# RWKV-7 pairs in a hybrid layer: gram results and chain outputs kept twice, block matrices of a pair in 64 columns, their products per head in quarters of TensorE's array

## Chip, cores, metric

One core of one Trainium2 chip. The metric is the device time of one execution in microseconds (us). Three executions of the kernel before took 2756.22, 2758.50 and 2762.81 us; the median, 2758.5 us, is the number to compare with.

## What is computed

One layer of a streaming encoder for two groups of frames: 528 prompt frames (16 learned ones and 512) and 64 sample frames. Cut to what matters here:

```
h    = rmsnorm(x);  proj = h @ w_in              # 2048 -> 5936 columns
ya   = rwkv7_mix(proj[:, :3360])                 # 16 heads of 64, this change
yb   = mamba2_mix(proj[:, 3360:])
x    = x + [ya, yb] @ w_out
x    = x + (silu(h2 @ w_gate) * (h2 @ w_up)) @ w_down     # h2 = rmsnorm(x)

def step(S, (r, w, k, v, kk, ka)):               # rwkv7, per head, S is 64 x 64
    sa = S @ kk
    S  = S * w - outer(sa, ka) + outer(v, k)
    return S, S @ r
y = group_norm(y) * lnx_w + lnx_b + (sum(r*k*r_k) * v);  ya = y * g
```

The kernel does the recurrence in 10 chunks of 64 frames. Inside a chunk the steps depend on each other through a unit lower triangular 64x64 matrix, which is inverted; between chunks only S is handed on.

## The kernel before, in words

Big products (projections, output, feed-forward) are split products in fp32r: each 128x128 weight block is multiplied three times (high by high, high by low, low by high). A projected tile of 128 columns is 96 matmuls of 296 columns (`in_tile`, line 367), called mk (k), mr (r), mv (v), mz, mB, mC, mx, then mwo for `w_out`. Two tiles at a time have a slot of two banks, so a tile can begin only when the tile two before it has been taken out of its banks. The small products of the recurrence share three spare banks (`get`, line 250), and the chain has one of its own.

Beside these tiles run the small f32 products of the recurrence, one *pair* of heads at a time, pairs 0 to 7. The steps of pair j:

- `pre_r` (line 789) makes the decayed factors `KB` and `ST`; then 20 gram products gr of 64x128 by 64x128 (10 chunks, 2 heads). `gram_out` (line 770) masks and copies each: into `ST`, into the block matrices `GB`, the diagonal 32x32 blocks into `NX`, the off-diagonal ones into `NS`.
- the inversion of the 32x32 blocks: VectorE transposes `NX` to `NN` (128x1024, line 830), GpSimd runs 62 TENSOR_TENSOR steps, VectorE transposes the result to `Zc` (128x352, line 883). `ZM` and `YB` lie in the memory of `NN`.
- `solved` (line 880): products pm of `NS` by `ZM` join the halves; copies build the block matrices `Zd` and `MB`.
- `applied` (line 918): products pb = `Zd` by `GB`, a copy, products px = `MB` by that; the result goes to `PT` for the chain. `steps` (line 855) transposes `KB` (tr) into `GB` and `yb`.
- `chain` (line 984): 10 chunks one after the other; in each a product pair p with `ST`, copies, a product pair p with `PT`, updates; the output goes to `Y`.
- `post` (line 1034): group norm of `Y`, transposes into `yb`, gate.

All block matrices are [128 partitions, 10 chunks, 128 columns] with the two heads on the diagonal and zeros beside it, so one 128x128 product does both heads.

The order of all instructions on each engine is made while the program is built: every step is a generator, `beat` (line 215) advances those whose inputs a clock of the planner (`tick`, line 136, with a cost per operation in `Timed`) holds ready, and marks such as ("px", j, g) hold a step back. The engines then run their queues strictly in that order. Where the planner's clock and the chip differ, an engine waits at the head of its queue.

Of the kernel before, what the change touches and what calls it, by code (L numbers as in the profile page):

```python
# [17 lines left out]
P = 128  # L18
# [68 lines left out]
def tile_hybrid(ctx, tc, xt, wq, wg, wd, lrw, cst, vec, s0w, s0m, y_out, sh_out, wkv_out, cv_out, sm_out):  # L87
# [61 lines left out]
    class Timed:  # L149
# [5 lines left out]
        def __getattr__(self, op):  # L155
            f, e = getattr(self.eng, op), self.e

            def call(out, *a, **k):
                r = f(out, *a, **k)  # L159
                part = 0.1 * (out.shape[0] <= 64)  # L160
                if e == "PE":
                    n = out.free_size()
                    tick(e, n / 2400 + 0.0133 if a[1].dtype == F32R else 0.175 if op == "transpose" else max(0.218, 0.15 + n / 1100))
                else:
# [506 lines left out]
    pos_zv = pos[0]  # L671
    R, ses, MVs, st_o = {}, [], [], []
    hrow = [slice(0, 64), slice(64, 128)]
    vrow = [slice(64, 128), slice(0, 64)]

    def A2():
# [4 lines left out]
        R["KB"] = al2(1280, NC, P)  # L681
        R["GB"] = al2(1280, NC, P)
        R["NS"] = al2(640, 5, P)
        R["NX"] = al2(1024, 32, 32)
# [7 lines left out]
        MVs.append(al2(2 * NC))  # L692
        R["Y"] = al2(TR)
        ses.extend(al2(64) for _ in range(2))
        R["zd"] = p2[0]
        R["Zd"], R["MB"] = al2(1280, NC, P), al2(1280, NC, P)
        R["XX"] = al2(388)
        st_o.extend(al2(64) for _ in range(2))
        G.memset(R["NX"], 0.0)
        G.memset(R["NS"], 0.0)  # L700
        G.memset(R["Zd"], 0.0)
        unit()
        G.tensor_scalar(R["MB"], cc("idn").unsqueeze(1).broadcast_to([P, NC, P]), 1.0, None, ALU.mult)
        for h in range(2):
# [65 lines left out]
    def gram_out(j, h, c0, n, b, pg):  # L770

        yield "VA"
        gb_, st, kx = R["GB"], R["ST"][j % 2][h], 64 * h
        q, m = vrow[h], cc("m3")[:, 64 - 64 * h:192 - 64 * h]
# [6 lines left out]
        A.copy(R["NX"][hi, c0:c0 + n, :], pg[hi, 0:n, hi])  # L781
        A.copy(R["NS"][lo, c0 // 2:(c0 + n) // 2, hi], pg[lo, 0:n:2, hi])
        A.copy(R["NS"][hi, c0 // 2:(c0 + n) // 2, lo], pg[lo, 1:n:2, hi])
        put(b)
# [4 lines left out]
    def pre_r(j):  # L789
# [65 lines left out]
    def steps(j):  # L855
# [4 lines left out]
        for c0, n in groups:  # L860
            b = yield from get()
            pg = bank(b, f"tr{j}{c0}").rearrange("p (c x) -> p c x", x=P)
            for c in range(c0, c0 + n):
                PE.transpose(pg[:, c - c0, :], R["KB"][:, c, :], cc("idn"))
            if c0 == 8:
                mark(("Tm", j))
            yield "A"
            for h in range(2):
                A.copy(R["GB"][hrow[h], c0:c0 + n, hrow[h]], pg[hrow[h], 0:n, hrow[h]])
# [10 lines left out]
    def solved(j):  # L880
# [16 lines left out]
        for c in range(5):  # L897
            PE.matmul(pm[:, c, :], R["NS"][:, c, :], R["ZM"][:, c], start=True, stop=True)
        aside()
        for q in range(4):  # L900
            d = slice(32 * q, 32 * q + 32)
            for e, i0, i1, g in ((V, 0, 10, 3), (V, 10, 11, 2)):
                e.tensor_copy(R["Zd"][d, :, 32 * q + 3 * i0:32 * q + 3 * i0 + g * (i1 - i0)].rearrange("p c (i g) -> p c i g", g=g),
                              Zc[d, i0:i1, 0:10 * g].rearrange("p i (g c) -> p c i g", g=g))
        cur[0].aside = False
        yield "A"
        for h in range(2):
            lo, hi = slice(64 * h, 64 * h + 32), slice(64 * h + 32, 64 * h + 64)
            for par, q in enumerate((hi, lo)):
                A.activation(R["MB"][hi, par::2, lo], pm[q, :, 0:32], AF.Copy, scale=-1.0)  # L910
        put(b)
# [6 lines left out]
    def applied(j, g, c0, n):  # L918
# [115 lines left out]
    def post(j):  # L1034

        Y, MV, bon = c3(R["Y"]), MVs[0], bons[j % 2]
        yield from until(("post", j - 1), then="V")
# [6 lines left out]
        yield "A"  # L1044
        A.activation(yb, R["Y"], AF.Square)
        yield "V"
# [1118 lines left out]
```

## Time and profile before

| what | us |
|---|---|
| median of 3 executions | 2758.5 |
| the profiled execution, its own time | 2759.7 |
| its span in the trace | 2757.6 |
| TensorE busy in the span | 2646.3 (96%) |
| VectorE busy | 2187.0 (79%) |
| ScalarE / GpSimd busy | 1405.1 / 385.9 |

How to read it: the recurrence runs beside the projection tiles from about 155 to 840 us. Behind it come the Mamba part, `w_out` (from 1009 us) and the feed-forward part, which the change does not touch. A busy share of the whole span says little of the stretch in which the pairs run, so that one is read by itself.

### The profile page before, as it was taken

To read this page: it belongs to the slowest core of one execution; us is meant where nothing else is said; L and a number is where in the kernel's file an instruction comes from. 1 tells how busy PE (TensorE), PEld (TensorE's weight loads), DVE (VectorE), ACT (ScalarE), POOL (GpSimd) and SP (SyncE) were. 2 spreads that over 40 slices of the span, in tenths; PEclk is the share of its full clock that TensorE was granted. 3 is DMA by queue.
4 is the path that set the end of the run, shared out by engine and by line. 5 is a ranking of instruction groups with operands and counts; after the bars stand their busy time and mean duration, and the time that the engine had idled before them with its cause. 6 is when DMAs were issued, how large, how long until landed. Compare 5 with 4: busy or idle time off the path is not lost.

```text
span 2757.6 us, 51938 instructions
## 1 busy us (share of the span) xinstructions
PE 2646.3 (96%) x19236; PEld 2580.2 (94%) x19236; DVE 2187.0 (79%) x4216; ACT 1405.1 (51%) x3013; POOL 385.9 (14%) x673
## 2 busy tenths in 40 slices
PE   8998899989999999999999999999999989999997
PEld 7888789988998989999999999999999989999997
DVE  7675787878878675568898888889888868888885
ACT  5645565656555453454454444545444434444544
POOL 3224334443401120120000000000000000000004
PEclk9999799999999999999999999999999999999999
DMA  5421121222222344343344444444344385654623
GB/s 182 171 71 54 52 71 58 67 62 74 61 88 86 92 145 132 114 146 122 124 159 132 151 133 142 144 146 145 131 152 130 123 275 194 218 186 156 203 71 108
DMA packets 196461, 349.57 MB, mean 127 GB/s; under 512 B 26096, under 2 KB 102000, under 8 KB 196080
## 3 DMA queue, kind: packets, MB, share of 16 engines
q1 hardware_dynamic: 196208, 346.26, 39.0%
q8 instruction: 151, 2.47, 0.4%
q14 instruction: 102, 0.84, 0.1%
HBM read 281.13 MB, written 65.06 MB: 126 GB/s over the span
## 4 chain that ended last, share of the span: by engine, by line
PE 79%; DVE 5%; ACT 5%; POOL 3%; issue 2%; DMA 2%; DVEq 0%; SPq 0%; ACTq 0%; POOLq 0%
PE y L159 15%; PE a L159 14%; PE r L159 14%; PE x L159 7%; PE mwo L159 7%; DVE mem L159 4%; POOL mem L159 3%; PE mx L159 3%; ACT mem L159 3%; PE mv L159 3%; PE mk L159 2%; PE mr L159 2%; PE mz L159 2%; PE p L159 2%; PE me L159 2%
## 5 line engine op out<-in xcount | busy, mean ns | idle before, releaser
L159 ACT CAST memr<-mem 128x512 fp32r<-128x512 f32 (+2 forms) x1230 | 714.1, 586 | 900.2 <-PE y L159 208.2
L159 DVE TENSOR_TENSOR memr<-mem,memr 128x512 fp32r<-128x512 f32 (+2 forms) x1076 | 691.8, 648 | 262.0 <-ACT memr L159 257.4
L159 DVE TENSOR_TENSOR mem<-mem 128x576 f32<-128x576 f32 (+9 forms) x1016 | 696.9, 702 | 21.7 <-DMA mem<-x1d 10.8
L159 POOL TENSOR_TENSOR mem<-mem 128x84 f32<-128x84 f32 (+28 forms) x583 | 337.0, 579 | 2218.8 <-ACT mem L159 1553.8
L159 ACT ACTIVATE mem<-mem 64x64 f32<-64x64 f32 (+12 forms) x413 | 217.1, 534 | 174.6 <-DVE mem L159 155.1
L159 PE MATMUL y<-memr 128*128 128x288 f32 x1352 | 206.6, 300 | 15.3 <-DVE mem L159 15.3
L159 PE MATMUL mwo<-memr 128*128 128x288 f32 x1536 | 210.4, 298 | 0.0
L159 PEld LDWEIGHTS mwo<-memr 128*128 128x128 f32 x1536 | 205.9, 189 | 3.0 <-issue 2.5
L159 PEld LDWEIGHTS y<-memr 128*128 128x128 f32 x1352 | 192.2, 192 | 15.9 <-issue 15.9
L159 PE MATMUL r<-ffm,memr 128*128 128x288 f32 x1348 | 202.7, 297 | 1.6 <-DMA ffm<-pd 1.1
L159 PE MATMUL x<-memr 128*128 128x288 f32 x1352 | 201.4, 295 | 0.0
L159 PE MATMUL y<-ffm,memr 128*128 128x288 f32 x1356 | 201.2, 295 | 0.2
L159 PE MATMUL a<-memr 128*128 128x288 f32 x1352 | 199.7, 294 | 1.2 <-DVE memr L159 1.2
L159 PE MATMUL r<-memr 128*128 128x288 f32 x1352 | 199.1, 294 | 0.0
L159 PE MATMUL a<-ffm,memr 128*128 128x288 f32 x1328 | 197.1, 295 | 0.0
L159 PEld LDWEIGHTS r<-ffm,memr 128*128 128x128 f32 x1348 | 188.3, 190 | 2.8 <-ACT ffm L159 1.3
L159 PEld LDWEIGHTS y<-ffm,memr 128*128 128x128 f32 x1356 | 187.7, 188 | 0.7 <-DMA ffm<-pd 0.4
L159 PEld LDWEIGHTS a<-memr 128*128 128x128 f32 x1352 | 186.9, 188 | 1.4 <-DVE memr L159 1.4
L159 PEld LDWEIGHTS x<-memr 128*128 128x128 f32 x1352 | 187.8, 188 | 0.0
L159 PEld LDWEIGHTS r<-memr 128*128 128x128 f32 x1352 | 186.2, 188 | 0.0
L159 PEld LDWEIGHTS a<-ffm,memr 128*128 128x128 f32 x1328 | 183.9, 188 | 0.0
L159 PE MATMUL mk<-memr 128*128 128x296 f32 x768 | 125.3, 313 | 4.6 <-DVE mem L159 4.6
(184 smaller groups left out, 4051.6 us busy)
## 6 DMA issues: line engine op xcount, KB each, us to landing
mem<-in_wg SPq DMA_DIRECT2D x176, 512.0 KB, 3.4
mem<-in_wq SPq DMA_DIRECT2D x268, 256.0 KB, 2.7
mem<-in_wd SPq DMA_DIRECT2D x128, 320.0 KB, 3.3
pd<-mem SPq DMA_DIRECT2D x280, 144.0 KB, 2.0
memr<-pd SPq DMA_DIRECT2D x80, 288.0 KB, 6.3
ffm<-pd SPq DMA_DIRECT2D x60, 288.0 KB, 6.6
mem<-lrd SPq DMA_DIRECT2D x16, 320.0 KB, 3.8
mem<-in_xt SPq DMA_DIRECT2D x16, 296.0 KB, 5.7
```

The costliest lines, as they stand in the source:

```text
L159: r = f(out, *a, **k)
```

## The change

- `GB` and `NS` exist twice, taken by j mod 2. `pre_r` starts the grams of pair j when the transpose of `NX` of pair j-1 is issued (a new mark, "nt") and the products pb of pair j-2 are done; before, it waited for the products px of pair j-1.
- `Y` exists twice (the second is the old buffer `rs`). `chain` j waits for `chain` j-2's normalised output and for the last chunk of chain j-1; before, for the normalised output of j-1. `post` loads its gate into `bon` behind the addition that reads `bon`; before, into `rs` ahead of it.
- `Zd`, `MB`, `NS` are packed into 64 columns, each head's block in its own 64 partitions. The products pm, pb and px are issued per head: 64 rows by 64 columns of the array, 20, 20+20... in place of 10, 10, 10 per pair (pm: 5 to 10, pb: 10 to 20, px: 10 to 20).
- The planner's price of an f32 product whose stationary operand has 64 partitions is multiplied by 0.6; that holds for gr too.

```diff
-                    tick(e, ... max(0.218, 0.15 + n / 1100))
+                    tick(e, ... max(0.218, 0.15 + n / 1100) * (0.6 if a[0].shape[0] == 64 else 1))
...
-        R["GB"] = al2(1280, NC, P)
-        R["NS"] = al2(640, 5, P)
+        R["GB"] = [al2(1280, NC, P)]
+        R["NS"] = [al2(320, 5, 64) for _ in range(2)]
...
-        R["Y"] = al2(TR)
+        Ys.extend((al2(TR), rs))
...
-        R["Zd"], R["MB"] = al2(1280, NC, P), al2(1280, NC, P)
+        R["GB"].append(al2(1280, NC, P))
+        R["Zd"], R["MB"] = al2(640, NC, 64), al2(640, NC, 64)
...
-        yield from until(*[("px", j - 1, g) for g in range(3)], then="P")
+        yield from until(("nt", j - 1), *[("py", j - 2, g) for g in range(3)], then="P")
         for h in range(2):
...
         yield from until(*[("px", j - 1, g) for g in range(3)], then="V")
         V.transpose(NN, NX.rearrange("p c t -> p t c"))
+        mark(("nt", j))
...
         for c in range(5):
-            PE.matmul(pm[:, c, :], R["NS"][:, c, :], R["ZM"][:, c], start=True, stop=True)
+            for q in hrow:
+                PE.matmul(pm[q, c, :], R["NS"][j % 2][q, c, :], R["ZM"][q, c], start=True, stop=True)
...
         for c in range(c0, c0 + n):
-            PE.matmul(pg[:, c - c0, :], R["Zd"][:, c, :], R["GB"][:, c, :], start=True, stop=True)
+            for q in hrow:
+                PE.matmul(pg[q, c - c0, :], R["Zd"][q, c, :], R["GB"][j % 2][q, c, :], start=True, stop=True)
         mark(("py", j, g))
...
         for c in range(c0, c0 + n):
-            PE.matmul(pg[:, c - c0, :], R["MB"][:, c, :], yb_[:, c - c0, :], start=True, stop=True)
+            for q in hrow:
+                PE.matmul(pg[q, c - c0, :], R["MB"][q, c, :], yb_[q, c - c0, :], start=True, stop=True)
...
-        yield from until(("chain", j - 1), ("pb", j), ("v", j), ("T", j))
-        EC, st, Y = ECs[j % 3], R["ST"][j % 2], c3(R["Y"])
+        yield from until(("chain", j - 2), ("cl", j - 1), ("pb", j), ("v", j), ("T", j))
+        EC, st, Y = ECs[j % 3], R["ST"][j % 2], c3(Ys[j % 2])
...
-        load(rs, LRD[j, 2][:, 0:TR])
         V.tensor_scalar(yb, yb, vv("lw", j), vv("lb", j), ALU.mult, ALU.add)
         yield "V"
         V.tensor_tensor(yb, yb, bon, ALU.add)
+        load(bon, LRD[j, 2][:, 0:TR])
         yield "V"
-        V.tensor_tensor(yb, yb, rs, ALU.mult)
+        V.tensor_tensor(yb, yb, bon, ALU.mult)
```

The rest of the diff is the same buffers under `j % 2` and marks for pairs -1 and -2.

**VectorE, around the end of pair 0's inversion.** In the kernel before (gr10.. are the gram results of pair 1, p10 the chain of pair 0, the 128x352 transpose makes `Zc` of pair 0):

```order
L159 STREAM_TRANSPOSE mem2_1443<-mem2_1443 128x352
L159 COPY mem2_1443<-mem2_1443 32x165 x2
L159 TENSOR_TENSOR memr_62<-mem_61,memr_62 128x512
...
L159 TENSOR_TENSOR mem2_1443<-gr100_2345,mem_61 64x512
L159 TENSOR_TENSOR mem2_1443<-gr100_2345,mem_61 64x4x64
L159 TENSOR_TENSOR mem2_1443<-gr104_2354,mem_61 64x512
L159 TENSOR_TENSOR mem2_1443<-gr104_2354,mem_61 64x4x64
L159 TENSOR_TENSOR mem_61<-mv10_2174,mem_61 128x64
```

and in the changed kernel:

```order
L159 TENSOR_TENSOR mem2_1443<-gr100_2059,mem_61 64x512
L159 TENSOR_TENSOR mem2_1443<-gr100_2059,mem_61 64x4x64
...
L159 TENSOR_TENSOR mem2_1443<-gr118_2202,mem_61 64x256
L159 TENSOR_TENSOR mem2_1443<-gr118_2202,mem_61 64x2x64
L159 TENSOR_TENSOR mem_61<-mz50_2034,mem_61 128x296
L159 TENSOR_TENSOR mem_61<-mz51_2035,mem_61 128x296
...
L159 STREAM_TRANSPOSE mem2_1443<-mem2_1443 128x352
```

All gram results of pair 1 now stand ahead of the `Zc` transpose of pair 0; before, all stood behind it.

**TensorE, between the tiles mz4 and mv5.** In the kernel before:

```order
L159 MATMUL mz41_5275<-memr_62 128x296
L159 MATMUL p14_5496<-mem_61,mem2_1443 128x64 x2
L159 MATMUL gr508_5506<-mem2_1443 128x128 x2
...
L159 MATMUL tr50_5577<-mem_61,mem2_1443 128x128 x4
L159 MATMUL mv50_5591<-memr_62 128x296
```

and in the changed kernel (the beginning and the end of that stretch):

```order
L159 MATMUL mz41_5314<-memr_62 128x296
L159 MATMUL pm4_5486<-mem2_1443 64x33 x10
L159 MATMUL pb40_5509<-mem2_1443 64x128 x8
L159 MATMUL pb44_5518<-mem2_1443 64x128 x8
L159 MATMUL px40_5532<-mem2_1443 64x128 x8
L159 MATMUL px44_5544<-mem2_1443 64x128 x8
L159 MATMUL pb48_5553<-mem2_1443 64x128 x4
L159 MATMUL px48_5571<-mem2_1443 64x128 x4
...
L159 MATMUL p14_5583<-mem_61,mem2_1443 128x64 x2
L159 MATMUL bs50_5828<-mem_61 128x320
L159 MATMUL mv50_5830<-memr_62 128x296
```

26 small products stood between the two tiles; now there are 103, with all of pm, pb and px of pair 4 and 22 products of its chain. At the stretch between mv2 and mk4 it is the other way round: 63 before, 22 now.

## Rows read from the trace of the kernel before

**Rows 1.** The page's busy times of TensorE and VectorE in the span, and TensorE's granted clock in 40 slices of 69 us (tenths).

```profile
PE 2646.3 (96%) x19236; PEld 2580.2 (94%) x19236; DVE 2187.0 (79%) x4216; ACT 1405.1 (51%) x3013; POOL 385.9 (14%) x673
...
PEclk9999799999999999999999999999999999999999
```

**Rows 2.** GpSimd in order of time: the 62 steps of the inversion, pair by pair (start, length, in brackets the idle time before).

```profile
194.10 37.05 POOL L159 TENSOR_TENSOR mem<-mem 128x31 f32<-128x31 f32 x62 [45.05 <-DVE mem L159]
267.82 31.15 POOL L159 TENSOR_TENSOR mem<-mem 128x31 f32<-128x31 f32 x62 [35.20 <-DVE mem L159]
732.11 32.26 POOL L159 TENSOR_TENSOR mem<-mem 128x31 f32<-128x31 f32 x62 [35.03 <-DVE mem L159]
```

**Rows 3.** Busy time of the engines in the eight stretches from the `NN` transpose to the `Zc` transpose of a pair (pairs 0, 1 and 4, and the sum of all eight; start, end, length, then TensorE, weight loads, VectorE, ScalarE, GpSimd, granted clock).

```profile
191.90:231.20 39.30, 33.06 (x233) 32.02 (x232) 25.80 (x38) 15.76 (x30) 32.27 (x62) 0.97 0.30 92
265.60:299.70 34.10, 33.37 (x246) 32.02 (x245) 24.68 (x58) 16.32 (x48) 26.36 (x62) 1.00 0.21 56
498.90:536.40 37.50, 37.34 (x280) 36.29 (x279) 30.48 (x71) 20.12 (x58) 30.62 (x62) 1.00 0.18 52
sum 294.20, PE 282.32 PEld 270.31 DVE 217.25 ACT 144.77 POOL 231.04; mean PE 35.29 PEld 33.79 DVE 27.16 ACT 18.10 POOL 28.88
```

**Rows 4.** The same for the seven stretches between them, from the `Zc` transpose of a pair to the `NN` transpose of the next (the first, the second, the fifth, and the sum of all seven).

```profile
231.20:265.60 34.40, 32.19 (x218) 30.25 (x218) 16.23 (x42) 19.62 (x61) 0.74 (x2) 0.88 0.12 33
299.70:337.50 37.80, 30.05 (x156) 25.59 (x155) 31.63 (x66) 26.57 (x69) 0.74 (x2) 0.69 0.16 51
536.40:583.00 46.60, 38.75 (x258) 35.19 (x256) 36.40 (x76) 31.61 (x82) 0.73 (x2) 0.85 0.23 70
sum 278.30, PE 250.33 PEld 228.47 DVE 222.19 ACT 192.95 POOL 5.81; mean PE 35.76 PEld 32.64 DVE 31.74 ACT 27.56 POOL 0.83
```

**Rows 5.** VectorE's costliest forms from 150 to 770 us (busy us, mean ns of one, idle time before).

```profile
L159 DVE TENSOR_TENSOR memr<-mem,memr 128x512 fp32r<-128x512 f32 x106 | 75.2, 712 | 29.5 <-ACT memr L159 28.6
L159 DVE STREAM_TRANSPOSE mem<-mem 32x320 f32<-32x320 f32 x104 | 51.9, 499 | 2.0
L159 DVE TENSOR_TENSOR mem<-mem 64x640 f32<-64x640 f32 x62 | 51.4, 835 | 0.9
L159 DVE TENSOR_TENSOR mem<-gr,mem 64x512 f32<-64x512 f32 x32 | 22.0, 688 | 14.3 <-PE gr L159 13.9
L159 DVE TENSOR_TENSOR mem<-gr,mem 64x256 f32<-64x256 f32 x48 | 20.3, 422 | 3.4 <-PE gr L159 2.7
```

**Rows 6.** TensorE in order of time, pair 0: the end of pb and px, and the first grams of pair 1.

```profile
232.83 2.31 PE L159 MATMUL pm<-mem 128*128 128x33 f32 x10 [7.88 <-ACT mem L159]
241.16 1.95 PE L159 MATMUL px<-mem 128*128 128x128 f32 x16
242.94 0.61 PE L159 MATMUL pb<-mem 128*128 128x128 f32 x4
243.30 1.06 PE L159 MATMUL mv<-memr 128*128 128x296 f32 x6
244.20 0.61 PE L159 MATMUL px<-mem 128*128 128x128 f32 x4
245.55 1.16 PE L159 MATMUL gr<-mem 64*128 64x128 f32 x8
246.63 0.53 PE L159 MATMUL mv<-memr 128*128 128x296 f32 x2
247.09 1.16 PE L159 MATMUL gr<-mem 64*128 64x128 f32 x8
```

**Rows 7.** TensorE: two groups of gram products that follow each other, the first on one half of the rows, the second on the other; and a form with 112 and with 80 stationary columns (840 to 1060 us, count, busy, mean).

```profile
561.89 1.17 PE L159 MATMUL gr<-mem 64*128 64x128 f32 x12
562.99 0.66 PE L159 MATMUL p<-mem 128*128 128x64 f32 x4
...
L159 PE MATMUL yd<-mem 112*112 112x64 f32 x128 | 15.9, 286 | 4.6 <-DVE mem L159 4.6
L159 PE MATMUL yd<-mem 80*80 80x64 f32 x64 | 5.3, 236 | 1.2 <-DVE mem L159 1.1
```

**Rows 8.** TensorE between the tiles mv2 and mk4, the last and the first matmuls around it, and the last group before mv5.

```profile
305.49 1.07 PE L159 MATMUL mv<-memr 128*128 128x296 f32 x6
310.12 0.61 PE L159 MATMUL pb<-mem 128*128 128x128 f32 x4
313.77 0.85 PE L159 MATMUL px<-mem 128*128 128x128 f32 x4 [3.04 <-ACT mem L159]
342.17 0.99 PE L159 MATMUL mk<-memr 128*128 128x296 f32 x2 [0.15 <-DVE mem L159]
576.79 0.98 PE L159 MATMUL mv<-memr 128*128 128x296 f32 x2 [0.88 <-DVE mem L159]
```

**Rows 9.** VectorE: the tile mz4 is taken out of its banks, and mr6, whose banks mv5 needs.

```profile
563.65 0.83 DVE L159 TENSOR_TENSOR mem<-mz,mem 128x296 f32<-128x296 f32 x2
576.21 0.90 DVE L159 TENSOR_TENSOR mem<-mr,mem 128x64 f32<-128x64 f32 x3
```

**Rows 10.** TensorE in the Mamba part, around the first yd products behind mC1.

```profile
856.13 2.51 PE L159 MATMUL yd<-mem 112*112 112x64 f32 x16 [1.65 <-DVE mem L159]
860.53 0.90 PE L159 MATMUL mx<-memr 128*128 128x296 f32 x2 [1.89 <-DVE mem L159]
```

More of the change, by code (lines that the diff above doesn't have):

```diff
@@ L162, in call @@
                     n = out.free_size()
-                    tick(e, n / 2400 + 0.0133 if a[1].dtype == F32R else 0.175 if op == "transpose" else max(0.218, 0.15 + n / 1100))
+                    tick(e, n / 2400 + 0.0133 if a[1].dtype == F32R else 0.175 if op == "transpose" else max(0.218, 0.15 + n / 1100) * (0.6 if a[0].shape[0] == 64 else 1))
                 else:
@@ L671, in tile_hybrid @@
     pos_zv = pos[0]
-    R, ses, MVs, st_o = {}, [], [], []
+    R, ses, MVs, st_o, Ys = {}, [], [], [], []
     hrow = [slice(0, 64), slice(64, 128)]
@@ L699, in A2 @@
         G.memset(R["NX"], 0.0)
-        G.memset(R["NS"], 0.0)
+        for q in R["NS"]:
+            G.memset(q, 0.0)
         G.memset(R["Zd"], 0.0)
         unit()
-        G.tensor_scalar(R["MB"], cc("idn").unsqueeze(1).broadcast_to([P, NC, P]), 1.0, None, ALU.mult)
+        for q in hrow:
+            G.tensor_scalar(R["MB"][q], cc("idn")[q, q].unsqueeze(1).broadcast_to([64, NC, 64]), 1.0, None, ALU.mult)
         for h in range(2):
@@ L772, in gram_out @@
         yield "VA"
-        gb_, st, kx = R["GB"], R["ST"][j % 2][h], 64 * h
+        gb_, ns_, st, kx = R["GB"][j % 2], R["NS"][j % 2], R["ST"][j % 2][h], 64 * h
         q, m = vrow[h], cc("m3")[:, 64 - 64 * h:192 - 64 * h]
@@ L781, in gram_out @@
         A.copy(R["NX"][hi, c0:c0 + n, :], pg[hi, 0:n, hi])
-        A.copy(R["NS"][lo, c0 // 2:(c0 + n) // 2, hi], pg[lo, 0:n:2, hi])
-        A.copy(R["NS"][hi, c0 // 2:(c0 + n) // 2, lo], pg[lo, 1:n:2, hi])
+        A.copy(ns_[lo, c0 // 2:(c0 + n) // 2, 32:64], pg[lo, 0:n:2, hi])
+        A.copy(ns_[hi, c0 // 2:(c0 + n) // 2, 0:32], pg[lo, 1:n:2, hi])
         put(b)
@@ L868, in steps @@
             for h in range(2):
-                A.copy(R["GB"][hrow[h], c0:c0 + n, hrow[h]], pg[hrow[h], 0:n, hrow[h]])
+                A.copy(R["GB"][j % 2][hrow[h], c0:c0 + n, hrow[h]], pg[hrow[h], 0:n, hrow[h]])
             for h in range(2):
@@ L902, in solved @@
             for e, i0, i1, g in ((V, 0, 10, 3), (V, 10, 11, 2)):
-                e.tensor_copy(R["Zd"][d, :, 32 * q + 3 * i0:32 * q + 3 * i0 + g * (i1 - i0)].rearrange("p c (i g) -> p c i g", g=g),
+                e.tensor_copy(R["Zd"][d, :, 32 * (q % 2) + 3 * i0:32 * (q % 2) + 3 * i0 + g * (i1 - i0)].rearrange("p c (i g) -> p c i g", g=g),
                               Zc[d, i0:i1, 0:10 * g].rearrange("p i (g c) -> p c i g", g=g))
@@ L909, in solved @@
             for par, q in enumerate((hi, lo)):
-                A.activation(R["MB"][hi, par::2, lo], pm[q, :, 0:32], AF.Copy, scale=-1.0)
+                A.activation(R["MB"][hi, par::2, 0:32], pm[q, :, 0:32], AF.Copy, scale=-1.0)
         put(b)
@@ L933, in applied @@
         for c in range(c0, c0 + n):
-            PE.matmul(pg[:, c - c0, :], R["MB"][:, c, :], yb_[:, c - c0, :], start=True, stop=True)
+            for q in hrow:
+                PE.matmul(pg[q, c - c0, :], R["MB"][q, c, :], yb_[q, c - c0, :], start=True, stop=True)
         mark(("px", j, g))
@@ L1034, in post @@
     def post(j):
-        Y, MV, bon = c3(R["Y"]), MVs[0], bons[j % 2]
+        Y, MV, bon = c3(Ys[j % 2]), MVs[0], bons[j % 2]
         yield from until(("post", j - 1), then="V")
@@ L1044, in post @@
         yield "A"
-        A.activation(yb, R["Y"], AF.Square)
+        A.activation(yb, Ys[j % 2], AF.Square)
         yield "V"
@@ L1075, in tile_hybrid @@
         mark(("py", -1, g))
+        mark(("py", -2, g))
         mark(("px", -1, g))
-    for q in ("rk", "chain", "pb", "pre", "prek", "post", "kb", "T", "vd", "Tm", "cl"):
+    for q in ("rk", "chain", "pb", "pre", "prek", "post", "kb", "T", "vd", "Tm", "cl", "nt"):
         for i in (-1, -2):
```

## The prediction, made before the changed kernel ran

> **What bounds the kernel now.** I read the page first: TensorE is busy 96% of the span, VectorE 79%, and the granted clock is lowest in the slices from about 280 to 350 us [rows 1]. That is where the pairs run, so I then read GpSimd in order of time. It shows one inversion at a time, with a regular idle time of 35 to 45 us and always VectorE as the releaser [rows 2]. So the pairs follow each other in a fixed cycle, and I cut the stretch at two instructions of VectorE that each pair has once: the `NN` transpose, which starts the inversion, and the `Zc` transpose, which ends it. From the first `NN` (191.9 us) to the last `Zc` (764.4 us) that makes 572.5 us: 294.2 us in eight inversions [rows 3] and 278.3 us in the seven stretches between them [rows 4]. Two things are to be seen. In an inversion the time is GpSimd's (231.0 of 294.2 us busy; none is shorter than 34.1 us), while VectorE is busy for 217.3 us. Between them VectorE is the busiest beside TensorE: 222.2 of 278.3 us, and 36.4 of 46.6 us in the fifth. TensorE is busy 282.3 + 250.3 = 532.7 us of the 572.5, so it has 40 us left there. The cycle is therefore long because the inversion of pair j, then the copies, pm, pb, px and the grams of pair j+1 come one after the other: the first eight grams of pair 1 start at 245.55 us, 1.35 us behind the start of pair 0's last px group (244.20) [rows 6].
>
> **What the change could take away.** Grams of pair j+1 no longer wait for px of pair j. If their VectorE work moved into the inversion, the stretches between would shrink by what the grams cost VectorE. Whether it does is not a matter of the marks but of the order that the planner made, and there I counted, per stretch, VectorE's instructions with the mean duration of their form, of which the costliest stand in [rows 5]. In the order before, the counts of the eight inversions are 24.6, 24.0, 27.9, 27.4, 30.6, 28.1, 28.9, 24.0 (215.5 us) and of the seven stretches between 18.8, 34.3, 39.8, 40.3, 39.9, 38.2, 32.0 (243.3 us; more than the busy 222.2 since durations of neighbours overlap). In the changed order they are 29.6, 19.1, 25.0, 30.5, 21.5, 30.1, 26.9, 24.8 (207.5 us) and 11.7, 48.2, 43.1, 38.1, 39.1, 37.7, 35.2 (253.1 us). So only pair 1's grams move ahead of the `Zc` transpose of the pair before, as the first order rows show. For pairs 2 to 7 the grams' results still stand between `Zc` of pair j-1 and `NN` of pair j. They are held there by what was not doubled further: `ST` has two copies and waits for the chain of pair j-2, and the grams want the same three spare banks as pb and px.
>
> **The sum, by VectorE's cycle, against the profiled 2759.7 us.**
> - First stretch between: 34.4 us for a count of 18.8, so it waited [rows 4]. With a count of 11.7 it is bound by pm to px, which took from 232.83 to 244.81 us [rows 6]; with the 1.6 us from the `Zc` transpose (231.2) to pm, and some 0.9 us until the next `NN` transpose starts, that is 14.5 us. That is 19.9 us less.
> - The other six: 278.3 - 34.4 = 243.9 us for counts of 224.5, a factor of 1.086. New counts 241.4 by the same factor give 262.2 us: 18.3 us more.
> - The inversions: pair 1's was already at the 34.1 us floor. Pair 4's count falls from 30.6 to 21.5, so I let its 37.5 us fall to the floor: 3.4 us less. The others I leave.
> - Behind pm of pair 7: that product stands behind 3280 big matmuls before and behind 3272 now, so eight more are left, at 0.15 us each (mv x6 in 0.90 us) [rows 6]: 1.2 us more.
> - The first yd group of the Mamba part stood right behind mC1 and cost TensorE 1.65 + 1.89 us of waiting [rows 10]; it now stands 40 big matmuls later. I take half of that, 1.8 us less; below it could be nothing, above it the whole 3.5 us.
> - TensorE's own work. Quarters need the array in another tiling than the tiles around them. What such a visit costs the grams show: eight grams and two mv matmuls take 1.54 us (245.55 to 247.09), while at the prices around them (px x16 in 1.78 us, mv x6 in 0.90 us) they would take 0.89 + 0.30 = 1.19 us, so 0.35 us per visit [rows 6]. In the order the visits go from 45 to 75: 30 x 0.35 = 10.5 us. Against it pm gets cheaper. With 33 moving columns its price follows the stationary columns: yd takes 124 ns of busy time with 112 and 83 ns with 80 [rows 7], and the same slope gives about 62 ns at 64. Per pair ten records of 111 ns become ten of 62 ns in each head, side by side: 0.5 us less, 4 us in all. Net 6.5 us, in a stage in which TensorE has 40 of 572.5 us free. I charge half, 3.2 us; the ends are 0 and 6.5.
> - pb and px I cost at nothing more: two products on different rows of the array run side by side. In the group of 12 gram records that begins at 561.89 us the second head's start while the first's run, and all 12 leave in 1.10 us, with the change of tiling in it; one after the other at 111 ns they would need 1.33 us and the change on top [rows 7]. Quarters use different rows and different columns. If that cover is gone, it is the third rival.
> - The gate's load in `post` now follows the addition, so its landing is no longer hidden by two VectorE operations of some 0.8 us. Other steps' instructions stand between; the range takes 0 to 1.6 us per pair on VectorE, and I take 0, since `post` has no reader of that product in the cycle.
>
> Sum: -19.9 + 18.3 - 3.4 + 1.2 - 1.8 + 3.2 = -2.4 us, so 2757.3 us beside the profiled 2759.7. The profiled execution was 1.2 us above the median, so I predict **2756 us**. About 0.2% (5.5 us) is what a measurement of this kernel can tell from no change, so the forecast is no change.
>
> **Rivals.**
> 1. *The stretches between need less waiting, faster.* The grams made VectorE wait 13.9 + 2.7 us [rows 5], and the chains no longer wait for the group norm of the pair before. For it: those waits sit in the long stretches [rows 4]. Against: pairs 2 to 7 keep their place in the order, so the grams' waits stay likely. If the 16.6 us all go: 2756 - 17 = 2739 us.
> 2. *TensorE stalls between mz4 and mv5, slower.* mv5 needs the banks of mr6. Before, VectorE took mz4 out at 563.65 and mr6 at 576.21 us [rows 9], with a count of 9.5 us of work between them. Now the count is 35.2 us: the copies to `Zd`, the norm of pair 3, the decayed factors and the grams of pair 5 all stand ahead of mr6. At the same ratio (12.6 us for 9.5) that is 46 us without a big matmul, in which TensorE has 103 small products, some 16 us of work at 0.11 us a record: 30 us lost, where 15.5 - 5 = 10.5 us were lost. The stretch before mk4 gets better: 35.8 us (306.4 to 342.17) with 14 us of products in it [rows 8] becomes a count of 12.8 in place of 24.0 us, some 20 us with 4 us of products. Together that is 30 + 16 - 10.5 - 22 = 13.5 us more, and the 10.5 - 4 us of tiling are then not hidden: 2760 + 20 = 2780, less 1.2 us for the median, about 2779 us. It decides if TensorE, not VectorE's cycle, sets the pace: then what is lost there is not won back from the 40 free us. For it: TensorE is 93% busy in the stage. Against: VectorE would be working through that stall, so its cycle does not get longer by it.
> 3. *The quarters don't run side by side, slower.* Then 640 records of 111 ns stand where 320 stood: 35.5 us more of TensorE's work in pb and px. With half of it in TensorE's free time that is 18 us, else all: 2774 to 2792, say 2784 us. For it: the two grams that overlapped wrote two banks, and two quarters write the same bank, which no row shows. Against: they write different partitions of it. The Trainium skill, TensorEngine Tiling (Array Packing), section Gotcha 1: PSUM Pressure, says that different row tiles cannot access the same PSUM bank at once; by that rule the two heads' quarters take turns and this rival's time holds. The trace before neither confirms nor contradicts it.
>
> **How the numbers follow.** The forecast gets 0.50, with its own range 2748 to 2764 us; within it 0.17 falls below 2753, 0.26 between 2753 and 2764 and 0.07 above, as the sum lies on the faster side. Rival 1 gets 0.23, rival 2 0.16, rival 3 0.11. Faster: 0.17 + 0.23 = 0.40; the same: 0.26; slower: 0.07 + 0.16 + 0.11 = 0.34. The range 2733 to 2789 takes in the rivals' times with some 5 us beside them and leaves out a part of each end, less than 2 in 10.
>
> **What would show it.** Right: `NN` of pair 0 to `Zc` of pair 7 takes 560 to 580 us; the first stretch between is some 15 us, the second over 40; a stretch of over 35 us without a big matmul stands before mv5 and one of about 20 before mk4; a group pb x16 has become x32 in about the same 1.8 us. Wrong: pb x32 takes 3.5 us (rival 3); the seven stretches sum to under 265 us (rival 1); the 572.5 us grow by over 12 us with TensorE idle before mv5 (rival 2). If all stretches shrink together, the order was not what held the cycle, and the whole way of counting fails.

## The result: 1.0% slower, and the profile of the changed kernel

The changed kernel took 2786.7 us (median; 2784.5 to 2787.6), the kernel before 2760.7 us on the same chip. The medians give a ratio of 1.0094; the ratio on record, with its 95% interval, is 1.0101 [1.0088, 1.0115]. The forecast was no change, 2756 us. The profiled execution of the changed kernel took 2784.5 us, its span is 2782.7 us, 25.1 us more than before.

The page of the changed kernel, as in [rows 1]: busy times, and the granted clock in 40 slices.

```profile
PE 2665.5 (96%) x19636; PEld 2590.6 (93%) x19636; DVE 2186.3 (79%) x4216; ACT 1407.2 (51%) x3014; POOL 384.1 (14%) x675
...
PEclk9999889979999999999999999999999989999999
```

VectorE is as busy as before. TensorE is busy 19.2 us more and idle 5.9 us more. The granted clock is lower than before from 348 to 417 us and from 557 to 626 us, and a little higher from 278 to 348. The cut into stretches, as in [rows 3] (the inversions, pair 1 and the sum of eight) and then as in [rows 4] (the seven stretches between, each, and their sum):

```profile
240.40:275.90 35.50, 34.93 (x260) 33.71 (x260) 19.46 (x53) 17.70 (x51) 23.62 (x62) 1.00 0.20 54
...
sum 296.00, PE 285.79 PEld 273.99 DVE 210.91 ACT 159.03 POOL 231.79; mean PE 35.72 PEld 34.25 DVE 26.36 ACT 19.88 POOL 28.97
```

```profile
227.90:240.40 12.50, 12.01 (x140) 10.43 (x139) 9.39 (x19) 8.67 (x24) 0.79 (x2) 1.00 0.25 64
275.90:332.40 56.50, 48.39 (x350) 43.33 (x349) 44.27 (x101) 31.73 (x93) 0.73 (x2) 0.82 0.17 53
368.30:424.80 56.50, 49.73 (x325) 43.32 (x324) 40.04 (x87) 29.66 (x88) 0.73 (x2) 0.76 0.18 57
462.70:507.60 44.90, 42.43 (x337) 38.18 (x335) 34.74 (x67) 31.95 (x79) 0.87 (x2) 0.96 0.24 71
543.20:593.60 50.40, 35.05 (x221) 30.15 (x220) 36.58 (x81) 29.59 (x78) 1.06 (x2) 0.65 0.13 39
631.10:672.40 41.30, 39.05 (x326) 35.14 (x325) 34.74 (x75) 25.20 (x77) 0.72 (x2) 1.00 0.25 75
709.30:748.00 38.70, 37.73 (x323) 34.38 (x321) 32.54 (x72) 24.58 (x69) 0.73 (x2) 1.00 0.17 51
sum 300.80, PE 264.40 PEld 234.93 DVE 232.31 ACT 181.38 POOL 5.63; mean PE 37.77 PEld 33.56 DVE 33.19 ACT 25.91 POOL 0.81
```

From the first `NN` transpose (187.7 us) to the last `Zc` (784.5 us) it is 596.8 us, 24.3 more than the 572.5 before; what lies ahead of it got 4.2 us shorter and what lies behind 5.0 longer. So the loss lies in the cycle, in the stretches between: 300.8 against 278.3 us. The first fell to 12.5 us; two and three became the longest of all, 56.5 us each. VectorE is busy 10 us more there, and idle 68.5 in place of 56.1 us. What it waited for from the first `NN` to the last `Zc`, before and then changed (us in total, times, longest):

```profile
DVE mem L159 <- PE p L159: 36.8, 38, 2.5
DVE mem L159 <- ACT mem L159: 33.4, 31, 3.3
...
DVE mem L159 <- DMA mem<-lrd: 1.5, 3, 0.7
```

```profile
DVE mem L159 <- ACT mem L159: 52.8, 32, 5.3
DVE mem L159 <- PE p L159: 44.3, 36, 4.8
...
DVE mem L159 <- DMA mem<-lrd: 6.1, 4, 2.1
```

Two releasers grow, by 19.4 and 7.5 us. Most of both are round trips of the *chain*: a product p on TensorE, a hand-over by ScalarE, an update on VectorE, and back. The gate's load adds 4.6 us. So I read where each chain runs: its nine counted steps are the updates `mem<-p,mem,mem` 64x64. Before, the chains of pairs 1 and 2 ran from 336.5 to 371.5 and from 414.3 to 448.1 us, beside the inversions, with one step each ahead of the next `NN`: 35.0 and 33.8 us. In the changed kernel they begin at 305.2 and 393.8 us, 27 and 31 us ahead of the next `NN`, and take 50.0 and 52.0 us.

What such a step looks like, in the third stretch of the changed kernel, on VectorE (start, length, in brackets the idle time before):

```profile
401.67 0.60 DVE L159 SCALAR_TENSOR_TENSOR mem<-p,mem,mem 64x64 f32<-64x64 f32 x2 [1.52 <-PE p L159]
406.73 0.61 DVE L159 COPY mem<-p 64x128 f32<-64x128 f32 x2 [4.46 <-ACT mem L159]
407.37 1.12 DVE L159 TENSOR_TENSOR mem<-gr,mem 64x512 f32<-64x512 f32 x2
410.24 0.60 DVE L159 SCALAR_TENSOR_TENSOR mem<-p,mem,mem 64x64 f32<-64x64 f32 x2 [1.75 <-PE p L159]
```

and on TensorE and ScalarE meanwhile:

```profile
401.49 2.07 PE L159 MATMUL gr<-mem 64*128 64x128 f32 x8
403.50 1.43 PE L159 MATMUL bs<-mem 128*128 128x320 f32 x2
404.26 1.16 PE L159 MATMUL mv<-memr 128*128 128x296 f32 x2
405.22 0.95 PE L159 MATMUL p<-mem,mem 128*128 128x64 f32 x4
```

```profile
406.26 0.44 ACT L159 COPY mem<-p 64x64 f32<-64x64 f32 x2 [2.80 <-PE p L159]
```

VectorE's next instruction is the chain's copy, and behind it stand the grams that `NN` needs. The copy needs ScalarE, that needs the product p, and p stands behind grams, a bs group (other small products) and two mv on TensorE, at a granted clock of 0.50. So VectorE stands for 4.46 us. From 400 to 407 us it is busy 0.98 of 7.00 us.

### The profile page after: what moved, and what is told of

It is laid out like the page before. It is cut to its first block, busy times and chain, and to the rows that moved or that the text cites. A ratio compares the mean times of both kernels' runs of the same rounds, so it can differ in the third digit from the quotient of the medians.

```text
span 2782.7 us, 52739 instructions
## 1 busy us (share of the span) xinstructions
PE 2665.5 (96%) x19636; PEld 2590.6 (93%) x19636; DVE 2186.3 (79%) x4216; ACT 1407.2 (51%) x3014; POOL 384.1 (14%) x675
## 4 chain that ended last, share of the span: by engine, by line
PE 75%; DVE 8%; POOL 6%; ACT 4%; issue 3%; DMA 2%; SPq 0%; DVEq 0%; ACTq 0%; POOLq 0%
PE y L159 15%; PE a L159 14%; PE r L159 14%; PE x L159 7%; DVE mem L159 6%; PE mwo L159 6%; POOL mem L159 6%; PE mx L159 3%; ACT mem L159 2%; PE mv L159 2%; PE mk L159 2%; PE me L159 2%; PE mr L159 1%; PE p L159 1%; DVE memr L159 1%
## 5 line engine op out<-in xcount | busy, mean ns | idle before, releaser
L159 DVE TENSOR_TENSOR mem<-mem 128x1024 f32<-128x1024 f32 (+9 forms) x1008 | 690.8, 701 | 29.0 <-DMA mem<-x1d 10.7
L159 ACT ACTIVATE mem<-mem 64x64 f32<-64x64 f32 (+13 forms) x413 | 216.6, 533 | 201.4 <-DVE mem L159 179.3
L159 PEld LDWEIGHTS y<-ffm,memr 128*128 128x128 f32 x1356 | 187.7, 188 | 1.2 <-DMA ffm<-pd 0.7
L159 PE MATMUL mv<-memr 128*128 128x296 f32 x768 | 129.1, 318 | 3.4 <-DVE mem L159 3.4
## 6 DMA issues: line engine op xcount, KB each, us to landing
mem<-in_xt SPq DMA_DIRECT2D x16, 296.0 KB, 5.8
```

## The experiments

In all tables "chains 1, 2" are the lengths of the chains of pairs 1 and 2, "stretches" the sum of the seven from `Zc` to the next `NN`, and "last step" the last counted step of pair 7's chain, all from the profiled execution, in us. Before: 35.0, 33.8; 278.3; 839.6. Changed: 50.0, 52.0; 300.8; 857.8.

**First: which part.** The theories at the start were S (the stalls without big matmuls), Q (the products in quarters and their visits to the other tiling) and V (VectorE's cycle); from e5 on P (the place of the stall before mv5) and N (new work, wherever that stall stands: in e5 the quarters, from e6 on the second output's own edits).

e1, the planner's price for 64-row products as before; e3, grams wait for px of the pair before; e4, one chain output (the chain waits for the norm, the gate early in its own buffer). Lines are shortened to what differs:

```diff
e1 -max(0.218, 0.15 + n / 1100) * (0.6 if a[0].shape[0] == 64 else 1)
   +max(0.218, 0.15 + n / 1100)
e3 -until(("nt", j - 1), *[("py", j - 2, g) for g in range(3)], then="P")
   +until(*[("px", j - 1, g) for g in range(3)], then="P")
e4 -Ys.extend((al2(TR), rs))
   +Ys.extend([al2(TR)] * 2)
   -until(("chain", j - 2), ("cl", j - 1), ("pb", j), ("v", j), ("T", j))
   +until(("chain", j - 1), ("pb", j), ("v", j), ("T", j))
   -load(bon, LRD[j, 2][:, 0:TR])          # behind the addition
   +load(rs, LRD[j, 2][:, 0:TR])           # ahead of lw, lb
```

e2 is e1, e3 and e4 together: quarters and 64 columns alone. e5 is e1 and e4 together. e6 is the kernel before with e4's edit the other way round: the second output (with its late gate) alone.

> The changed kernel with the planner's old price (no factor 0.6), all else kept: two copies, 64 columns, quarters. Theory S (stall): what the change costs is TensorE's wait for the banks of the next tile, and it goes with the VectorE work that stands, in the order, between taking out the last tile and taking out the tile whose banks are needed next. Counted over the pairs' stage that is 52.7 us before, 71.7 us in the changed kernel, 32.5 us here. The change's 19 us of count cost 26 us, so 1.4 us per us: 20 us less than before gives about 28 us less, some 2733 us. Theory Q (tiling): the 30 more visits to another tiling cost the 26 us; here are 77 visits (75 in the changed kernel), so 2785 to 2790 us. Theory V (VectorE's cycle, as in the prediction): the counts give 569 us for the cycle, 3.6 us under the one before, about 2757 us.

> 64 columns and quarters alone: gram results, off-diagonal blocks and Y as in the kernel before (grams wait for px of the pair before, the chain for the norm before, second copies not needed), old price. 75 visits to another tiling, as in the changed kernel. Theory S: the count is 55.2 us against 52.7, so about 3 us more and 3 us for the tiling, some 2766 us. Theory Q: the whole 26 us, 2785 to 2790 us. Theory V: cycle 576 us, 2764 us.

> The changed kernel, but the grams of a pair wait for px of the pair before again (the second copies of the gram results are there and bring nothing). Theory S: the count is 58.6 us, 5.9 over before: about 8 us more, some 2768 to 2771 us. Theory Q: 73 visits, 2785 us. Theory V: cycle 582 us, 2770 us. If the early grams were what costs, this is the run that loses the 26 us; S says that it loses most of them, by its order alone.

> The changed kernel with one Y: the chain waits for the norm of the pair before, the gate is loaded into its own buffer early. Theory S: the count is 62.7 us, 10 over before: about 14 us more, some 2774 us. Theory Q: 74 visits, 2785 us. Theory V: cycle 571 us, 2759 us.

> The changed kernel with one Y and the planner's old price: of the change, quarters and two copies of the gram results are left. Theory P (place): the change's 26 us are one stall of TensorE's, in front of the tile mv5, which comes with the second Y; quarters and early grams by themselves cost under 5 us. Then this run stands with the one-Y run, 2750 to 2765 us. Theory N (new work): quarters cost some 20 us wherever they stand (as the run with quarters alone says, 2782), and early grams give back the 12 us that lie between the run whose grams wait (2798) and the changed kernel (2787): some 2770 us.

> The kernel before with the second Y alone (chain waits for the last chunk of the pair before and the norm of the one before that, the gate is loaded behind the addition). No quarters, no second gram results, old price. Theory P: the second Y costs by the stall that the order makes of it; here the order has 34 small products in front of mv5 (26 before, 103 in the changed kernel) and 57 in front of mk4 (63 before), so about the time before, 2755 to 2770 us. If the second Y costs by itself what lies between one Y and two in the changed kernel (30 us): 2790 us.

| run | us | ratio [95%] | chains 1, 2 | stretches | last step |
|---|---|---|---|---|---|
| e1 old price | 2768.7 | 1.0027 [1.0015, 1.0038] | 36.5, 38.2 | 295.6 | 838.4 |
| e2 quarters alone | 2782.2 | 1.0079 [1.0062, 1.0096] | 35.2, 44.9 | 309.0 | 853.9 |
| e3 grams wait | 2798.3 | 1.0134 [1.0119, 1.015] | 34.3, 34.3 | 330.8 | 875.7 |
| e4 one output | 2756.1 | 0.9978 [0.9968, 0.9988] | 33.7, 29.9 | 290.7 | 844.1 |
| e5 one output, old price | 2763.1 | 1.0009 [0.9998, 1.002] | 34.7, 35.8 | 294.6 | 841.8 |
| e6 second output alone | 2785.5 | 1.0103 [1.0082, 1.0123] | 33.3, 36.2 | 327.5 | 882.6 |

The part that costs is the second output: without it the change is 0.2% *faster* than before (e4), with nothing else it is 1.0% slower (e6; its profiled execution took 2793.1 us, so its stretches are read a little long). It does not cost alike in every order: with the old price and both outputs the loss is 0.27% (e1). The early grams do pay: 12 us (e3 against the change) and 19 us (e2 against e5). Q fell: e4 has 74 visits to the other tiling, the change 75, the kernel before 45. Yet quarters alone are 0.8% slower than before (e2), with the same visits, and why was not followed. No theory foresaw the times of e1 to e4: V came near in e4 alone (2759 us), Q in e2 alone (2785 to 2790), S in none. N's 2770 us for e5 was missed, where P's range held; in e6 it was N that came near.

**Is it the stall before mv5?** It came as rival 2 had it. Changed kernel: the last group of mz4, mv5's first (TensorE), mr6 taken out (VectorE), and that stretch:

```profile
541.91 5.70 PE L159 MATMUL mz<-memr 128*128 128x296 f32 x40
...
599.23 0.99 PE L159 MATMUL mv<-memr 128*128 128x296 f32 x2 [0.73 <-DVE mem L159]
```

```profile
598.66 0.89 DVE L159 TENSOR_TENSOR mem<-mr,mem 128x64 f32<-128x64 f32 x3
```

```profile
547.60:599.20 51.60, 34.20 (x199) 28.11 (x198) 36.62 (x80) 30.48 (x85) 2.86 (x9) 0.60 0.12 38
```

51.6 us without a big matmul against 15.5 before, at a granted clock of 0.60. e7 lets tile v5 take whichever of the two slots is free first; e8 is e4 with that rule for all tiles:

```diff
         s = mt[0] % nslots
         mt[0] += 1
+        if nslots == 2 and name == "v5":
+            stall(lambda: all(slots.get(q) == "busy" for q in (0, 1)), name)
+            s = min((q for q in (0, 1) if slots.get(q) != "busy"), key=lambda q: slots.get(q, 0.0))
         stall(lambda: slots.get(s) == "busy", name)
```

> The changed kernel, but the tile mv5 takes the slot that is free first (that of mz4) and not the one of mr6, which waits for VectorE. Up to the end of mz4 all orders are the same. Theory P: the stall of 51 us in front of mv5 falls to under 10 us; at the start of mk7 the kernel is 15 to 30 us ahead of the changed kernel (619.7 us). Behind it the order has another stretch of 66 small products, in front of mz7, that may take back half: 2765 to 2775 us. Theory N: the stall is only where new work shows, and the time stays within 5 us of 2787.

> The changed kernel with one Y, and every tile of the projections takes whichever slot is free first. In the order no stretch in front of a tile has over 24 small products but the chain's own. Theory P: no stall in front of a tile, so faster than before, 2735 to 2750 us. Theory N: 2756 (the one-Y run) or more.

e7: 2788.9 us, 1.0111 [1.0094, 1.0127]; mv5 begins at 551.0 us, 48 us sooner, and the time is that of the change. Chains 1 and 2 are unchanged, 50.0 and 52.0 us. The lead was given back at the tiles behind: mB begins 18 us ahead of the changed kernel (703.7 against 722.0 us), the first mx 2 us behind it. But e7 did not take such stretches away: two others came, of 27.8 us ahead of a mz and 14.4 ahead of a mC. Stretches of over 6 us without a big matmul, from 187 to 900 us, sum to 74.1 us in e7 and 83.5 in the changed kernel. What speaks against S and P is that this sum does not go with the time: it is 78.2 us in the kernel before and 29.4 us in e5, which takes as long. e8, made to have no long stretch ahead of a tile: 2785.3 us, 1.0104 [1.0083, 1.0125], 29 us slower than e4 and far from P's 2735 to 2750. So theories S and P fell; N is left, and what in it.

**Late gate, or early chain?** Two things come with the second output: the gate is loaded late (theory G), and the chain starts without the norm before it, ahead of the next `NN` (theory C). e9 is e4 and e10 the kernel before with the late load alone. e11 (the change) and e12 (e6) hold every chain behind the next `NN`:

```diff
e9, e10
+        load(bon, LRD[j, 2][:, 0:TR])      # behind the addition, in place of rs ahead of lw, lb
e11, e12
-        yield from until(("chain", j - 2), ("cl", j - 1), ("pb", j), ("v", j), ("T", j))
+        yield from until(("chain", j - 2), ("cl", j - 1), ("pb", j), ("v", j), ("T", j),
+                         *([("nt", j + 1)] if j + 1 < NPAIR else []))
```

> The kernel with one chain output (2756 us, the chain waits for the norm before it) with only the gate's load moved behind the bonus addition into the bonus's buffer, as the change has it. Theory G (the second output costs because it takes the gate's buffer: the gate then comes late, VectorE stands for its DMA at the end of every norm, 6.1 us in the changed kernel, and all that is queued behind stands with it): 2770 to 2788 us. Theory C (the second output costs because the chain, freed from the norm before it, starts ahead of the next pair's NN transpose, 17 of its 72 counted steps there against 8 before and 12 with one output, and each step is a round trip for which VectorE waits in order): 2756 to 2766 us, chain steps ahead of NN about 12.

> The kernel before with the late gate load alone (into the bonus's buffer, behind the addition); one output, chain waits for the norm. G: most of the +26 us that the second output with its late gate cost the kernel before, so 2774 to 2788 us. C: the waits on the DMA alone, 0 to 6 us more than before, 2759 to 2767 us.

> The changed kernel, two outputs and late gate kept, with one wait more: the chain of pair j also waits until the NN transpose of pair j+1 is issued. No chain step can then lie between Zc of a pair and the next NN. C: VectorE's stretches between fall from 300.8 us to 290 or less and the time to 2755 to 2768 us. G: the late gate stays, 2780 to 2792 us.

> The kernel before with the second output and the late gate (2785.5 us, 18 chain steps ahead of NN), and the same wait: the chain of pair j behind NN of pair j+1. C: stretches between from 327.5 us to under 300, 2755 to 2770 us. G: 2780 us or more.

| run | us | ratio [95%] | chains 1, 2 | stretches | last step |
|---|---|---|---|---|---|
| e9 one output, late gate | 2765.4 | 1.0009 [0.9997, 1.002] | 34.3, 29.2 | 282.1 | 844.9 |
| e10 before, late gate | 2782.5 | 1.0074 [1.0052, 1.0096] | 32.3, 39.7 | 315.4 | 867.1 |
| e11 change, chains held | 2757.5 | 0.9985 [0.9973, 0.9997] | 31.4, 30.7 | 285.1 | 839.2 |
| e12 e6, chains held | 2786.0 | 1.0085 [1.0065, 1.0106] | 30.1, 29.0 | 310.9 | 868.4 |

With the change, C is right: holding the chains takes the whole loss away, with both outputs and the late gate kept, and the late gate costs 9 us by itself (e9 against e4). With the grams, products and price of the kernel before, G's numbers came: the late gate alone costs 22 us, and holding wins nothing. G's mechanism is not shown by that. VectorE only waits 5 us more for the gate's DMA there; by count its queue holds 476 in place of 459 us of work from `NN` of pair 0 to `Zc` of pair 7, so the new order also moved other work into the cycle. What costs the rest stays open.

**Which chains.** e13 holds those of pairs 1 and 2, e14 of 4 to 6, e16 of 1, 2 and 4, e17 of 1 to 4. e15 is e4 with all held.

```diff
-        *([("nt", j + 1)] if j + 1 < NPAIR else []))
+        *([("nt", j + 1)] if j in (1, 2) else []))      # e14 (4, 5, 6); e16 (1, 2, 4); e17 (1, 2, 3, 4)
```

> The changed kernel with the chains of pairs 1 and 2 alone held behind the NN transpose of the next pair: the two that started 27 and 31 us ahead of it and took 50 and 52 us for their steps, against 29 to 41 us for the others. C (the early chains cost by their place): stretches two and three fall from 56.5 us each to 39 to 47, as with all chains held (45.1 and 39.5), and the time to 2758 to 2772 us. R (the run with all chains held was another order that happened to fall well, and no place is to blame): nothing says which half of it, the time anywhere from 2765 to 2795 us, and chains 1 and 2 not above 35 us long would go with no gain.

> The changed kernel with the chains of pairs 4, 5 and 6 alone held: they had 3, 2 and 2 steps ahead of NN and were 41.0, 40.7 and 38.8 us long. C: stretches two and three stay at 56.5, the gain is the smaller part, 0 to 10 us, so 2776 to 2787 us. R: anywhere from 2765 to 2795 us.

> The changed kernel with one output, the gate early in a buffer of its own and every chain held behind the next NN. If place of the chain and late gate add up: below both 2756 us (one output) and 2757.5 us (two outputs, held), 2742 to 2755 us. If holding and one output are two ways to the same thing (the chain does not start early): 2753 to 2762 us.

> The changed kernel with the chains of pairs 1, 2 and 4 held. With 1 and 2 alone held (2752.6 us) the chain of pair 4 had become the early one: 50.4 us long, four steps ahead of NN, stretch five at 56.0 us. C: that chain falls to under 35 us, stretch five below 52, and the time to 2742 to 2752 us. K (once the early chains are held, VectorE's count sets the stretches again: counts of the last six now 255.6 against 247.8, at the 1.106 that the last run had): 8.6 us more in the stretches, 2756 to 2768 us.

> The changed kernel with the chains of pairs 1 to 4 held. C: as with 1, 2 and 4 held, 2742 to 2752 us. K: counts of 247.0 in place of 247.8, so no change against 1 and 2 alone, 2749 to 2757 us.

| run | us | ratio [95%] | chains 1, 2 | stretches | last step |
|---|---|---|---|---|---|
| e13 held 1, 2 | 2752.6 | 0.9976 [0.9967, 0.9985] | 31.3, 30.9 | 286.6 | 832.8 |
| e14 held 4 to 6 | 2778.8 | 1.0080 [1.0060, 1.0099] | 49.8, 51.7 | 308.2 | 868.9 |
| e15 one output, all held | 2779.8 | 1.0079 [1.0064, 1.0094] | 29.7, 33.1 | 291.7 | 861.3 |
| e16 held 1, 2, 4 | 2751.6 | 0.9966 [0.9953, 0.9979] | 31.4, 30.7 | 292.3 | 836.2 |
| e17 held 1 to 4 | 2753.1 | 0.9973 [0.9962, 0.9984] | 31.4, 30.7 | 279.2 | 823.7 |

The two long chains are the cause in the changed kernel: holding them alone brings 34 us, more than C foresaw (2758 to 2772), and a kernel 0.24% faster than before; holding the later ones brings 8 at most. e13's stretches two and three:

```profile
276.40:321.40 45.00, 35.30 (x293) 31.37 (x291) 39.22 (x82) 28.88 (x72) 0.73 (x2) 0.88 0.21 64
356.50:396.20 39.70, 34.69 (x285) 30.33 (x284) 35.76 (x73) 23.73 (x66) 0.73 (x2) 0.91 0.21 61
```

84.7 us in place of 113.0: VectorE is busy 9.3 us less (the steps went beside the inversion, where GpSimd's time covers them) and idle 9.7 in place of 28.7 us. Of that idle time the chain's two releasers, p and ScalarE's mem, had 21.5 us in the changed kernel and 1.0 us in e13. Of the 32.5 us that the span got shorter, 17.4 lie in the cycle and 15.6 behind the last `Zc`. A chain step there on VectorE:

```profile
408.01 0.58 DVE L159 SCALAR_TENSOR_TENSOR mem<-p,mem,mem 64x64 f32<-64x64 f32 x2
408.51 0.60 DVE L159 TENSOR_TENSOR mem<-p,mem 64x128 f32<-64x128 f32 x2
409.04 1.66 DVE L159 SCALAR_TENSOR_TENSOR mem<-mem 128x640 f32<-128x640 f32 x2
411.40 0.60 DVE L159 SCALAR_TENSOR_TENSOR mem<-p,mem,mem 64x64 f32<-64x64 f32 x2 [0.69 <-PE p L159]
```

3.4 us from step to step, where the early chain took 8 to 9. Two things differ: the place and the clock. In e13 the granted clock is 1.00 from 408 us on, while those three early steps of the changed kernel (401.67 and 410.24 us are two of their ends) ran at 0.50 until 418 us. The early chain's fourth step, still ahead of `NN` and at full clock, took 3.5 us. But chain 4 of e13 has early steps of 8.4 and 6.4 us at full clock, with other work of VectorE between them. So a step can be long by its place alone, and no run says how much of the 8 to 9 us is the clock's.

Holding more chains wins nothing clear: in e16 K foresaw the stretches (last six 279.8 us for a count of 255.6) and missed the time (2751.6, C's range by its edge); in e17 K's range held. e15 missed both expectations: with one output and held chains, each chain waits for `NN` and for the norm before it, and pair 7's begins 55 us behind its `Zc` (41 us in e11). Of all kernels here, those up to 2769 us have their last chain step at 824 to 845 us, those from 2778 us on at 852 to 883.

**What stays open.** Early and long chains of pairs 1 and 2 are what the changed kernel pays for, but they are not the only way to lose such a time, and not every early chain is a loss. e2, e3, e6, e8, e10, e12 and e15 took 2780 to 2798 us with chains 1 and 2 of at most 45 us, in e8, e12 and e15 with no step ahead of `NN`. In e13 the chain of pair 4 is early and 50.4 us long, with four steps ahead of `NN`, and the kernel is faster than before; holding that chain too (e16) wins 1 us by the medians, 3 by the ratios. VectorE stood only 5.7 us for that chain's two releasers in the stretch, and TensorE kept its clock (0.95):

```profile
516.80:572.70 55.90, 52.22 (x406) 47.72 (x405) 44.01 (x94) 32.08 (x91) 0.73 (x2) 0.95 0.24 76
```

In stretches two and three of the changed kernel VectorE stood 21.5 us for them, and the clock was 0.82 and 0.76. The mean granted clock of the profiled executions parts the two groups as the last step does: 0.964 to 0.972 from 2778 us on, 0.973 to 0.977 up to 2769 us (before, changed, e13):

```profile
core 0: 2757.6 us, clock 0.974
core 0: 2782.7 us, clock 0.968
core 0: 2750.2 us, clock 0.977
```

With two levels, 0.50 and 1.00, that is some 143, 178 and 127 us at the lower one. Eight grams take 2.07 us there and 1.16 at full clock (below), so the 35 us more of the changed kernel are worth up to some 15 of its 25 us, an estimate from these rows. In the stretch read below TensorE waited before the clock fell, so the clock need not be a cause of its own; no run holds it fixed, and its share stays open.

## Why the prediction was wrong, point by point

The frame held: 24.3 of the 25.1 us lie between the first `NN` and the last `Zc`, and the first stretch fell by 21.9 us (19.9 forecast). The forecast had taken it from rows of which the first, up to 239 us, ran at a granted clock of 0.50 [rows 6]; in the changed kernel that stretch has 1.00.

**The step that failed is "the other six ... by the same factor give 262.2 us".** The order was counted rightly and the factor was wrong: 288.3 us for a count of 241.4 is 1.194, not 1.086. That is 26.1 us, nearly the whole miss of 27.5 us (2.4 us less forecast, 25.1 more measured). The factor is no constant of the engine; it holds waiting in it, and the place of a chain is one thing that decides how much. By stretch, for two and three: changed 56.5/48.2 = 1.17 and 56.5/43.1 = 1.31, together 13.8 of the 26.1 us; with the two chains held 45.0/42.4 = 1.06 and 39.7/38.0 = 1.04. Most of the rest is in stretch five, 50.4/39.1 = 1.29, with three steps of chain 4 ahead of `NN`, and in stretch four, 44.9/38.1 = 1.18, with none of chain 3, so that one the early chain does not explain. For the last six: 1.106 in e13, 1.102 in e11, 1.080 in e17. With the early chains held the factor of before is a fair one again in these three. The prediction had the order in which it could have been seen: it counted the work in a stretch, not the round trips in it.

- *Rival 1* took the opposite side of the same edit: "the chains no longer wait for the group norm". That wait was the thing that kept the chain behind the grams. VectorE did wait less for grams (7.5 in place of 12.2 us) and more for chains.
- *Rival 2*: its stall came (51.6 us; 46 forecast), and so did the shorter one before mk4 (17 us, some 20 forecast). That stall is not what is paid: in e7 it is gone and the time is the same. What it says of TensorE setting the pace is not refuted: of the 25.1 us, TensorE is busy for 19.2, with hardly more work and a lower clock.
- *Rival 3*: fell. pb and px of pair 0 in the changed kernel, as in [rows 6], and pm ahead of them:

```profile
230.28 0.74 PE L159 MATMUL pm<-mem 64*64 64x33 f32 x18 [0.20 <-DVE mem L159]
...
236.32 1.96 PE L159 MATMUL px<-mem 64*64 64x128 f32 x32
238.12 0.60 PE L159 MATMUL pb<-mem 64*64 64x128 f32 x8
```

  32 quarters px take 1.96 us where 16 full products took 1.95; pb x32 takes 2.37 us in pair 0 and 1.96 in pair 3, where 16 took 1.95 to 2.22. The Trainium skill, TensorEngine Tiling (Array Packing), section Gotcha 1: PSUM Pressure, says that different row tiles cannot access the same PSUM bank at once; the measurement decides, and here two quarters on different rows and columns wrote one bank at no loss in px.
- *The inversions*: 296.0 us, 5.2 over the forecast. Pair 4's fell to 35.6, not to the floor of 34.1.
- *Tiling visits*: 3.2 us charged. No run has the visits alone: e4 with 74 is faster than before, but with the early grams; e2 with 75 and without them is slower. So the term is neither borne out nor refuted.
- *pm*, forecast 0.5 us a pair cheaper: its 20 quarters take 1.20 or 1.21 us from first to last in five of the eight pairs, its 10 full products took 1.20 us in five. So nothing was won there; in pair 0 two quarters went ahead and the other 18 waited for VectorE.
- *The yd hole*: the yd products waited 5.3 us for VectorE where [rows 7] has 5.8; 1.8 us were forecast.
- *The gate's load*: taken at 0, range 0 to 12.8 us in eight pairs. It is 9 us (e9 against e4): VectorE stands 6.1 us for loads of that tensor (lrd) in the changed kernel, 1.5 before. That "`post` has no reader of that product in the cycle" was no reason to take 0: what stands behind the load in VectorE's queue is in the cycle.

The range held the time, but by luck: 2786.7 us lies near its end, which was put there for the prices of rivals 2 and 3 (2779 and 2784 us), and neither came true as it was told. The side of the forecast was wrong.

## What to carry to other kernels

When a wait is taken away from a chain of round trips, ask where in the other engines' queues its steps will now stand: a serial chain that moves from beside a long-running engine into the stretch that this engine waits for can put its round trips into the cycle, as those of pairs 1 and 2 here. Ask too what the other engines have to do there: the early chain 4 in e13 cost nothing that shows, with other work for VectorE between its steps and TensorE's clock at 0.95. Buffers that let a step start sooner are only worth it where sooner is better; with one wait that holds it (here on `NN` of the next pair, for two pairs) the loss became a small gain. And a measured ratio of elapsed time to counted work may be carried over only while the kind of work in the stretch stays the same; count the round trips apart.

## What the runs showed of the hardware that was not expected

- Two 64x64 quarters of one product pair, in one bank, start 6 to 8 ns apart, and the next such pair starts some 109 ns behind them (px at 236.32 us, granted clock 1.00); a full product had 111 ns (px x16 in 1.78 us [rows 6]).
- pm with 64 stationary columns per head, at full clock: 18 records in 0.74 us, some 57 ns from one pair to the next. With 128 columns it is 102 ns from record to record at full clock (the kernel before, pair 1, the line below). The 2.31 us for 10 in [rows 6] are no measure of it: there the granted clock was 0.50, and a record took 213 ns.

```profile
304.45 1.20 PE L159 MATMUL pm<-mem 128*128 128x33 f32 x10
```

- In the third stretch of the changed kernel the clock fell while TensorE waited for a busy VectorE, and then VectorE waited for a slower TensorE. It fell at 391 us: from 388 to 400 us TensorE was busy 6.45 of 12.00 us and VectorE 11.39. From 400 to 407 us TensorE is busy throughout at 0.50, the lower of its two levels (1.2 GHz), eight grams take 2.07 us, where at full clock they take 1.16 [rows 6], and now it is VectorE that stands. The clock rose at 418 us.

```profile
388.00:394.00 6.00, 3.08 (x14) 2.16 (x14) 5.46 (x13) 2.15 (x9) 0.00 (x0) 0.75 0.60 213
394.00:400.00 6.00, 3.37 (x11) 2.17 (x10) 5.93 (x14) 2.54 (x11) 0.00 (x0) 0.50 0.17 56
```

```profile
400.00:407.00 7.00, 7.00 (x26) 6.06 (x27) 0.98 (x4) 2.66 (x11) 0.00 (x0) 0.50 0.00 0
```
